# A small load, read by nothing, issued on SP just ahead of the last store

## The chip, the cores and the metric

The kernel runs on one core of one Trainium2 chip. The metric is device time in microseconds (us) per execution. Most figures below are medians of several executions; single traces are named as such. Every execution quoted here is of the fast state. The ratio of two kernels is the mean time of one kernel's fast runs over that of the other's of the same rounds, so it is not quite the ratio of the medians quoted beside it. SP, DVE and ACT are the engines SyncE, VectorE and ScalarE. In the traces a transfer shows as packets and as sixteen completions on its semaphore (the store of the kernel before: 144 packets, completions from 82.429 to 82.597 us); it is counted as landed at the last of the sixteen.

## The reference

```python
batch, dim = 1024, 4096          # x and y: float32
def reference(x, y, axis):       # axis = -1
    return np.sum((x - y) ** 2, axis=axis).astype(np.float32)
```

33.5 MB are read, 4 KB are written: 1024 sums, which stand as 8 sums on each of 128 partitions.

## The kernel before

SP issues all transfers. The two inputs are loaded in slices that get smaller towards the end; DVE subtracts, ACT squares and sums, and the very last 128 columns are squared and summed on DVE. When DVE has reduced the last partial sums (semaphore `sums`), SP stores all 1024 results in one transfer, clears the semaphores while it is under way (81.577 to 81.645 us in the trace, with the store landing at 82.597), and waits for it (semaphore `stored`). Shortened, with comments added:

```python
class Program:
    ...
    def close(self, engine, stored, value):
        engine.sem_clear(range(self.sems[0].num, self.sems[-1].num + 1))
        engine.wait_ge(stored, value).then_inc(stored, -value)
...
    for j, (c0, c1) in enumerate(ys):
        final = j == len(ys) - 1
        wait_loaded(c1, landed_y[j][1])
        for piece in pieces_of(j, c0, c1):
            sub(*piece)                                   # DVE, then_inc(diffs, 1)
            if final:
                nc.vector.wait_ge(diffs, n["diffs"])
                nc.vector.tensor_tensor_reduce(...).then_inc(sums, 1)
                ...
            square(*piece, where[piece])                  # ACT
    ...
    complete(7)                                           # DVE reduce, then_inc(sums, 1)

    nc.sync.wait_ge(sums, n["sums"])
    nc.sync.dma_start(out=ov, in_=results).then_inc(stored, 16)
    prog.close(nc.sync, stored, 16)
```

## Time and profile before

| What | us | From |
|---|---|---|
| median of the first three executions | 83.98 (83.97 to 84.12) | times |
| span of the profiled execution | 82.63 | trace |
| last load landed | 80.251 | semaphore records |
| last sum ready | 81.161 | semaphore records |
| store issued | 81.177 to 81.525 | trace |
| store's first and last packet | 82.019, 82.213 | DMA packet records |
| store's last completion | 82.597 | semaphore records |

The table is read downwards: the last sum is ready, and the store takes 1.42 us from its issue to its last completion. The lines of the profile that show this stand in the prediction.

### The profile page before, as it was taken

How to read it: one execution, taken by the hardware profiler on the slowest of the kernel's cores; microseconds unless marked ns; L12 is line 12 of the kernel's file. 1: busy time of each engine (PE TensorE's matmuls, PEld its weight loads, DVE VectorE, ACT ScalarE, POOL GpSimd, SP SyncE). 2: the span in 40 equal slices, each digit the busy share in tenths (PEclk: the TensorE clock that was granted, in tenths of full speed). 3: DMA queues.
4: the chain of work that ended last, by engine and by line, in shares of the span. 5: the costliest groups of instructions: out<-in, count | busy, mean ns of one | idle time of the engine just before them, and what ended most of it. 6: DMA issues, size and time to landing. Idle time of an engine off the chain costs nothing.

```text
span 82.6 us, 136 instructions
## 1 busy us (share of the span) xinstructions
DVE 36.8 (45%) x27; ACT 33.4 (40%) x41; POOL 0.2 (0%) x4
## 2 busy tenths in 40 slices
DVE  0000000000000000000299999999189996989992
ACT  3300000000000000000000979889896999899991
POOL 0000000000000000000000000000000000000000
DMA  5998998888999991999599699969979799999960
GB/s 127 389 500 381 595 547 381 381 381 381 504 504 504 504 504 63 441 504 504 254 508 508 286 476 508 476 286 508 423 339 509 339 437 440 426 402 416 395 220 2
DMA packets 2736, 33.56 MB, mean 406 GB/s; under 512 B 432, under 2 KB 1328, under 8 KB 1712
## 3 DMA queue, kind: packets, MB, share of 16 engines
q1 hardware_dynamic: 2736, 33.56, 95.9%
HBM read 33.55 MB, written 0.00 MB: 406 GB/s over the span
## 4 chain that ended last, share of the span: by engine, by line
DMA 63%; SPq 16%; DVE 12%; ACT 4%; issue 1%
DMA Y<-in_y_dram 63%; SPq L108 16%; DVE X L175 11%; ACT X L181 4%; DVE Y L204 0%; DVE results L188 0%; SPq L220 0%; DVE results L204 0%
## 5 line engine op out<-in xcount | busy, mean ns | idle before, releaser
L175 DVE TENSOR_TENSOR X<-X,Y 128x2048 f32<-128x2048 f32 (+10 forms) x21 | 36.2, 1780 | 44.3 <-DMA Y<-in_y_dram 44.3
L181 ACT ACTIVATE X<-X 128x2048 f32<-128x2048 f32 (+9 forms) x20 | 31.2, 1559 | 46.1 <-DVE X L175 46.0
L181 ACT ACTIVATION_READ_ACCUMULATOR X<-X 128x1 f32 x20 | 3.7, 186 | 0.0
L181 ACT ACT_TABLE_LOAD x1 | 1.3, 1283 | 1.4 <-PEq L19 1.4
L188 DVE TENSOR_REDUCE results<-parts 128x1 f32<-128x2 f32 (+2 forms) x4 | 0.4, 152 | 0.0
L204 DVE CUSTOM_DVE_ANT_0 Y<-X,parts 128x128 f32<-128x128 f32 x1 | 0.4, 352 | 0.0
L250 POOL MEMSET const-bfloat16-1.0<- 128x1 bf16 x1 | 0.1, 101 | 0.0
L250 POOL MEMSET const-uint8-127<- 128x1 uint8 x1 | 0.1, 101 | 0.0
L250 POOL MEMSET const-float32-0.0<- 128x1 f32 x1 | 0.1, 98 | 0.2 <-issue 0.2
L250 POOL MEMSET const-float32-1.0<- 128x1 f32 x1 | 0.1, 98 | 0.0
L204 DVE DVE_READ_ACCUMULATOR2_ANT results<- 128x1 f32 x1 | 0.1, 83 | 0.0
## 6 DMA issues: line engine op xcount, KB each, us to landing
Y<-in_y_dram SPq DMA_DIRECT2D x1, 8128.0 KB, 39.0
X<-in_x_dram SPq DMA_DIRECT2D x1, 6144.0 KB, 20.2
X<-in_x_dram SPq DMA_DIRECT2D x1, 4096.0 KB, 48.3
Y<-in_y_dram SPq DMA_DIRECT2D x1, 4096.0 KB, 57.5
X<-in_x_dram SPq DMA_DIRECT2D x1, 2736.0 KB, 13.3
X<-in_x_dram SPq DMA_DIRECT2D x1, 2048.0 KB, 7.1
Y<-in_y_dram SPq DMA_DIRECT2D x1, 1392.0 KB, 19.0
Y<-in_y_dram SPq DMA_DIRECT2D x1, 1312.0 KB, 16.1
```

The costliest lines, as they stand in the source:

```text
L108: nc.sync.dma_start(out=dst[:, home(c0, c1)], in_=src[:, c0:c1]).then_inc(sem, 16)
L175: nc.vector.tensor_sub(out=a, in0=a, in1=Y[:, home(c0, c1)]).then_inc(diffs, 1)
L181: nc.scalar.activation(out=a, in_=a, func=Square, accum_out=acc).then_inc(acts, 1)
L188: nc.vector.tensor_reduce(out=results[:, r : r + 1], in_=parts_of(r, len(row_parts[r])), axis=mybir.AxisListType.X, op=add,).then_inc(sums, 1)
L204: nc.vector.tensor_tensor_reduce(out=Y[:, home(*piece)], in0=X[:, home(*piece)], in1=X[:, home(*piece)], scale=1.0, scalar=parts_of(r, 1), ...
L250: nc = _bacc.Bacc("TRN2", target_bir_lowering=False, num_devices=1)
```

## The change

The intent is to have the DMA queue at work just before the store that the kernel ends with, so that the store doesn't begin on a queue that has fallen idle (for 2.15 us in the trace of before, 79.872 to 82.019). SP waits for the last subtraction, issues a load of 32 bytes per partition into a buffer that nothing reads, and then waits for the sums as before. The load has a semaphore of its own, which is waited for and reset at the end.

```diff
+        self.own = []
...
         engine.sem_clear(range(self.sems[0].num, self.sems[-1].num + 1))
+        for sem in self.own:
+            engine.wait_ge(sem, value).then_inc(sem, -value)
         engine.wait_ge(stored, value).then_inc(stored, -value)
...
     stored = nc.alloc_semaphore("stored")
+    prog.own.append(nc.alloc_semaphore("ahead"))
...
+    ahead = nc.alloc_sbuf_tensor("ahead_home", [P, R], F32).ap()
+    nc.sync.wait_ge(diffs, n["diffs"])
+    nc.sync.dma_start(out=ahead, in_=xv[:, 0:R]).then_inc(prog.own[0], 16)
     nc.sync.wait_ge(sums, n["sums"])
     nc.sync.dma_start(out=ov, in_=results).then_inc(stored, 16)
```

## The prediction

> **What bounds the kernel now.** I read the page first (busy shares, the 40 slices), then the chain that ended last, then the timeline of the last three microseconds, the stretches of that tail, SP's own waits, and finally the single records of DMA packets and semaphore updates in the trace, because the chain stops before the store.
>
> From the page:
>
> ```profile
> DVE 36.8 (45%) x27; ACT 33.4 (40%) x41; POOL 0.2 (0%) x4
> ...
> DMA  5998998888999991999599699969979799999960
> ...
> q1 hardware_dynamic: 2736, 33.56, 95.9%
> ```
>
> The DMA row is full almost to the end, DVE and ACT are below half. The kernel is a stream of 33.55 MB at a mean of 406 GB/s; nothing that SP adds after the last load can touch that stream. Only the last two slices (2.07 us each) are not DMA-bound, and there the change sits.
>
> The end of the chain that ended last (start us, us, what):
>
> ```profile
> 66.94 13.12 DMA Y<-in_y_dram
> 80.05 0.02 issue
> 80.08 0.57 DVE X L175 x2
> 80.65 0.03 issue
> 80.67 0.35 DVE Y L204
> 81.03 0.01 DVE results L204
> 81.03 0.12 DVE results L188
> ```
>
> The last load lands at 80.05, two subtractions end at 80.65, a multiply-and-sum and a reduction follow. The chain leaves out the store; the timeline and the list of DMA issues have it:
>
> ```profile
> 81.18 0.35 SPq L232 DMA_DIRECT2D out_dram<-results  x1
> ```
> ```profile
> out_dram<-results SPq DMA_DIRECT2D x1, 4.0 KB, 1.4
> ```
>
> So the span of 82.63 us ends with 1.4 us of one 4 KB store. The stretches of the tail show that almost none of it is data (columns: stretch, its length, busy DVE, ACT, POOL, clock, DMA share, GB/s):
>
> ```profile
> 79.90:81.20 1.30, 1.18 (x6) 1.06 (x6) 0.00 (x0) 1.00 0.00 0
> 81.20:82.00 0.80, 0.00 (x0) 0.00 (x0) 0.00 (x0) 1.00 0.00 0
> 82.00:82.25 0.25, 0.00 (x0) 0.00 (x0) 0.00 (x0) 1.00 0.31 17
> 82.25:82.63 0.38, 0.00 (x0) 0.00 (x0) 0.00 (x0) 1.00 0.00 0
> ```
>
> The trace's records refine this. Last reduction's update 81.161; store issued 81.177 to 81.525; first of its 144 packets (128 of 32 B, 16 of 4 B) at 82.019, sixteen of them begun within 25 ns; last at 82.213; sixteen completions from 82.429 to 82.597; SP's closing wait passes at 82.613 and ends at 82.630. The store is therefore 0.842 us from issue to first packet, 0.20 us of packets, 0.38 us to the last completion. The DMA engines stood empty from 79.872 to 82.019, that is 2.15 us. The load can only help by shortening the 0.842 us: that is where a queue that has gone idle would pay.
>
> [...]
>
> **The change part by part.** It removes nothing. It adds on SP a wait for the last subtraction, one load issue of 4 KB (128 rows of 8 f32), and after the clearing of semaphores one more wait-and-subtract. It moves nothing.
>
> 1. The load's issue. The last subtraction's update comes at 80.648. SP took 16 ns from the sums' update (81.161) to the store's issue (81.177), so the load starts at about 80.664. What does an issue take? From the timeline:
>
> ```profile
> 53.45 0.33 SPq L108 DMA_DIRECT2D X<-in_x_dram  x1
> 53.82 0.91 SPq L108 DMA_DIRECT2D Y<-in_y_dram  x2
> 54.77 0.44 SPq L108 DMA_DIRECT2D X<-in_x_dram  x1
> ```
>
> One issue after a pause takes 0.33 us, the following ones 0.43 to 0.44, and they end about 0.48 us apart. [...] The load ends on SP at 80.664 + 0.33 = 80.99; with the 0.05 us that lie between two issues SP is at the store by 81.04, before the sums at 81.161. Slack 0.12 us; with 0.44 us instead, SP is ready at 81.15 and the slack is 10 ns.
>
> [...]
>
> 3. The load's packets. Issue to first packet as for the store, 0.84 us: 81.51. Packets 0.20 us if like the store's: 81.71. Completions up to 0.58 us after the first packet: about 82.09. The store's packets, due at 82.02, find an engine that finished the load's data 0.3 us before. So they do not collide[...].
>
> 4. The extra closing wait. SP clears semaphores at 81.577 to 81.645, then waits for the load (about 82.09) and then for the store (82.597). The first wait ends 0.5 us before the second could; its 17 ns and the gap are beside the store. Cost 0.
>
> 5. DVE and ACT: no instruction changed. The load writes a buffer of its own from 81.5 on, when both are done.
>
> Sum of the costs: 0 on the path. The gain is whatever part of 0.842 us belongs to an idle queue. What can it be? [...] 0.842 - 0.48 = 0.36 us remain, an upper bound. A second view: the very first load, at 0.00 us, with the queue unused before, has its first packet at 0.998, which is 0.156 us more than the store had after 2.15 us of pause. So a colder queue seems slower, but this shows only the step from unused to 2 us idle, not from 2 us to 0.3 us. I choose about a quarter of the 0.36 us, 0.08 us, as an estimate: no trace here shows that a gain of this kind exists, yet one piece of evidence leans that way.
>
> Predicted: 83.98 - 0.08 = 83.90 us.
>
> **The rivals.**
>
> - Nothing is cold. 0.842 us is the fixed length of an issue, and the store lands 1.4 us after 81.18 as before. For it: sixteen packets of the store begin within 25 ns[...]. Against it: the 0.998 us of the first load, whose packets also begin up to 0.5 us apart. Time 83.98, within the scatter of 83.97 to 84.12. This is the single most likely outcome.
> - The queue[...] is cold and the load wakes it. The store then starts 0.2 to 0.36 us earlier: 83.6 to 83.8. For it: 2.15 us of emptiness[...]. Against it: nothing in this trace shows a small DMA on a warm queue.
> - The load gets in the way. [...] the first packets of the first load took 0.92 to 1.43 us where the later ones of the same 16 KB took 0.611, so a first read can cost 0.3 to 0.8 us more. Added to the load's start at 81.51 this reaches 81.8 to 82.5, and the store would begin up to 0.3 us late after 82.02; the extra wait for the load would then also be close to the end. Time 84.1 to 84.3. Against it: those first packets met sixteen engines starting on 16 KB each at once, this load has 32 B each.
> - The load lands after the store and its wait becomes the end. It would need more than 1.93 us from 80.664 to 82.597, where the store needed 1.42. [...] time at most some 0.2 us more.
>
> **Range and chances.** The gain is bounded by 0.36 us and the plausible losses by about 0.3 us. I give the first rival some 45 in 100, a gain of over 0.1 us some 35, a loss of over 0.1 us some 20. The scatter between runs is up to 0.14 us. This gives 83.60 to 84.22 us. Two per cent are 1.68 us, more than the store's whole 1.4 us: faster by so much is practically excluded, 0.01; slower by so much would need an effect that nothing in the profile hints at, 0.015; within 2% 0.975.
>
> **What would show each step right or wrong.** In the profile of the changed kernel: a load issue on SP at 80.66 of about 0.33 us (step 1); the store's issue still 16 ns after the sums and 0.33 to 0.36 us long (steps 1 and 2), not 0.43 or later; a group of 144 packets between 81.5 and 81.75 that is separate from the store's (step 3); the load's wait closing before 82.2 (step 4). The verdict between the rivals is one number: the store's first packet relative to its issue. 0.84 us means that nothing was cold, 0.5 to 0.75 that the load woke the queue, more than 0.84 that it stands in the way. The prediction is wrong if the time leaves 83.60 to 84.22, and its reasoning is wrong, even inside the range, if the time moves while the store's issue-to-landing stays 1.4 us.

The forecast's sum came to 83.98 - 0.08 = 83.90 us: costs of 0 on the path, and a gain of 0.08 us as about a quarter of 0.842 - 0.48 = 0.36 us. Terms of this sum rested on mechanisms and figures that no trace shows: step 2 of the costs (expected delay 0, at worst some 0.1 us), the same delay among the losses of the third rival, and the reason for taking 0.48 us off the 0.842 us. What the trace shows of the 0.48 us is that the ends of successive issues lie so far apart; that every store has to wait so long before its first packet was my assumption.

## The result and the profile after

In the first comparison the changed kernel took 84.21 us (median of 6, 84.11 to 84.68) and the kernel before 84.06 us (median of 6, 83.97 to 84.12): ratio 1.0028, 95% interval 1.0005 to 1.0052. Predicted were 83.90 us and a small gain. There was no gain. The median lies just inside the upper end of the range, 84.22; the mean of the six, 84.29, lies outside. Of the 0.31 us between 83.90 and 84.21, 0.08 us are the gain that isn't there, 0.08 us the starting point (83.98 was a median of three executions, six gave 84.06), and 0.15 us the difference of this comparison.

The page of the changed kernel, its DMA row in 40 slices and its DMA queue:

```profile
DMA  5999999888999997599799979979999999999950
...
q1 hardware_dynamic: 2880, 33.56, 95.7%
```

The stream is as full as before (95.7% and 95.9% of the span); the 144 packets more are the small load. Next its timeline at the end, and the list of its DMA issues (KB each, us from issue to landing):

```profile
80.91 0.33 SPq L238 DMA_DIRECT2D ahead_home<-in_x_dram  x1
81.42 0.35 SPq L240 DMA_DIRECT2D out_dram<-results  x1
```
```profile
ahead_home<-in_x_dram SPq DMA_DIRECT2D x1, 4.0 KB, 1.7
out_dram<-results SPq DMA_DIRECT2D x1, 4.0 KB, 1.4
```

The load is where it was meant to be, and its issue takes 0.33 us. The store still needs 1.4 us; by the semaphore records it is 81.417 to 82.829, that is 1.412 us, against 1.420 before. The number that the prediction had named, issue to first packet, is 0.842 us as before. (The records don't name the transfer of a packet, and a few of the load's come late in this trace; n1_again below, where the two groups are apart, has 0.840 us.) The stretches of this tail (stretch, length, busy DVE, ACT, POOL, clock, DMA share, GB/s) have the same form as before, except that most of the small load's packets now lie in the first of them:

```profile
81.42:82.25 0.83, 0.00 (x0) 0.00 (x0) 0.00 (x0) 1.00 0.08 5
82.25:82.46 0.21, 0.00 (x0) 0.00 (x0) 0.00 (x0) 1.00 0.39 21
82.46:82.87 0.41, 0.00 (x0) 0.00 (x0) 0.00 (x0) 1.00 0.00 0
```

So where do the 0.23 us come from by which this span (82.863 us) is longer than that of before (82.630 us)? The chain that ended last answers, in its last pieces (start us, us, what):

```profile
67.24 13.06 DMA Y<-in_y_dram
...
80.32 0.57 DVE X L179 x2
...
81.28 0.11 DVE results L192
```

The last load lands at 80.30 here by this view and at 80.05 there, on the transfer that the chain follows (the last but one; the very last landed at 80.476 and 80.251). All that follows is shifted by that quarter of a microsecond. The small load is issued at 80.912, when the stream is done (last landing at 80.476); it can't have delayed it. One more sight of the profile matters, SP's own waits (line, what for, us, times, longest):

```profile
SPq L47 <- SPq L47: 0.8, 1, 0.8
...
SPq L48 <- SPq L48: 0.2, 1, 0.2
```

L47 is the new closing wait for the load, L48 the one for the store. SP waits 0.8 us for the load and then only 0.2 us for the store. The load is thus much closer to setting the end than the prediction had it: its last completion came at 82.644, the store's at 82.829.

### The profile page after: what moved, and what is told of

Read it like the earlier page. It is cut to its first block, busy times and chain, and to the rows that moved or that the text cites. A ratio compares the mean times of both kernels' runs of the same rounds, so it can differ in the third digit from the quotient of the medians.

```text
span 82.9 us, 138 instructions
## 1 busy us (share of the span) xinstructions
DVE 36.8 (44%) x27; ACT 33.4 (40%) x41; POOL 0.2 (0%) x4
## 3 DMA queue, kind: packets, MB, share of 16 engines
q1 hardware_dynamic: 2880, 33.56, 95.7%
## 4 chain that ended last, share of the span: by engine, by line
DMA 63%; SPq 16%; DVE 12%; ACT 4%; issue 1%
DMA Y<-in_y_dram 63%; SPq L112 16%; DVE X L179 11%; ACT X L185 4%; DVE Y L208 0%; DVE results L192 0%; SPq L224 0%; DVE results L208 0%
```

## The experiments

Three theories were put against each other. A: nothing was cold, the load is off the path, and the difference of the first comparison is scatter of the load stream. B: the shifted semaphore numbers or the layout of the program slow the stream. C: in some executions the small load lands after the store and sets the end.

### n0_numbers: the numbering alone

```diff
     stored = nc.alloc_semaphore("stored")
+    nc.alloc_semaphore("ahead")
...
+    nc.alloc_sbuf_tensor("ahead_home", [P, R], F32).ap()
     nc.sync.wait_ge(sums, n["sums"])
```

> The kernel before with the change's extra semaphore and extra buffer allocated, but no load and no wait. Theory A (the load is off the path; the 0.15 us between the medians is skew between the DMA engines that stands before any changed instruction and differs from execution to execution or chip to chip): ratio to before 1.000, within 0.001. Theory B (the shifted semaphore numbers or layout slow the load stream): ratio about 1.002 to 1.003, with the sixteen completions of the first load spread over some 0.55 us as in the profile of the changed kernel, not 0.23 us as in that of before. Theory C (the small load lands after the store in some executions): 1.000.

Measured: 84.09 us (84.05 to 84.24), before 84.06 us; ratio 1.0002, interval 0.9988 to 1.0015. Its trace has a wide spread in the first load's completions (0.521 us from the first to the last of the sixteen; 0.226 us in the trace of before, 0.577 us in that of the changed kernel) and a last load at 80.441 us, although the time equals that of before. So the late stream that I saw in the changed kernel's trace also comes in a kernel without the load, and the wide spread in it does not mark a slower kernel. No slowing by the numbers shows; an effect below about 0.15% would not be seen. The added instructions are not in this kernel; for them the repeats of the changed kernel stand.

### n1_again: the changed kernel on the same chip

No edit.

> The changed kernel again, on the same chip as the other runs of this call. Theory A: ratio 1.000 to 1.001, no skewed tail of slow executions, and the spread of the first load's completions as in the other runs of this chip. Theory B: 1.002 to 1.003 and a wide spread of 0.55 us, like n0_numbers. Theory C: 1.001 to 1.003 with single executions 0.3 to 0.6 us slow, while the quickest executions equal those of before; the small load's last completion within 0.2 us of the store's.

Measured: 84.15 us (83.95 to 84.38); ratio 1.0004, interval 0.9987 to 1.0021. The quickest execution, 83.95, is as quick as the kernel before on that chip (83.96), and the 0.28% did not come back. In this trace the packets of load and store are cleanly apart: the store's first is 0.840 us after its issue. The load's last completion lies 0.363 us ahead of the store's. One execution at 84.38 left theory C open.

### e1_early: the load two subtractions earlier

```diff
-    nc.sync.wait_ge(diffs, n["diffs"])
+    nc.sync.wait_ge(diffs, n["diffs"] - 2)
```

> The same load, issued two subtractions earlier, some 0.6 us sooner, so that its landing can't set the end. Issue to landing of the store stays 1.41 to 1.42 us in all theories but a warm queue. Theory A: 1.000. Theory B: 1.002 to 1.003, as n1_again. Theory C: 1.000, and without the slow executions that n1_again has.

Measured: 84.12 us (84.05 to 84.32); ratio 1.0006, interval 0.9991 to 1.0021. Store: 0.843 us to the first packet, 1.420 us to landing. The load itself was issued at 80.210, only 0.24 us after the last packet of the stream (79.971), and its first packet came 0.934 us after its issue; in the changed kernel, where the pause ahead of the load's issue was 0.75 us, it took 0.929 us. A shorter pause did not help the load.

### e2_two: two loads ahead of the store

```diff
     nc.sync.dma_start(out=ahead, in_=xv[:, 0:R]).then_inc(prog.own[0], 16)
+    nc.sync.dma_start(out=ahead2, in_=xv[:, R:2 * R]).then_inc(prog.own[1], 16)
```

(The second load has its own buffer and semaphore.)

> Two such loads one after the other before the store[...]. If[...] nothing is cold, the store's issue ends 0.44 us later than it would, its first packet stays 0.49 us after the end of the issue, and the time is 0.40 to 0.48 us more than before (ratio 1.005). If a queue with work standing on it starts the store sooner, the first packet comes less than 0.40 us after the end of the issue and the ratio is under 1.003. In theory C the second load, landing 1.73 us after an issue at 81.04, ends at 82.8 and still lies before the store.

(The 0.44 us expected here rest on the 0.48 us between the ends of successive issues in the trace of before.)

Measured: 84.59 us; ratio 1.0062, interval 1.0047 to 1.0077. The timeline of its end, and the store in its list of issues:

```profile
80.77 0.33 SPq L239 DMA_DIRECT2D ahead_home<-in_x_dram  x1
81.14 0.43 SPq L241 DMA_DIRECT2D ahead_home<-in_x_dram  x1
81.62 0.43 SPq L243 DMA_DIRECT2D out_dram<-results  x1
```
```profile
out_dram<-results SPq DMA_DIRECT2D x1, 4.0 KB, 1.6
```

Here is what was measured with work standing on the queue: the store's issue took 0.43 us, and the three issues ended 0.475 us apart (81.098, 81.573, 82.047 us). With the 0.926 us that lie between the last load's landing and the store's issue in the trace of before, this store would have been issued at 81.258 and done at 81.606; it is late by 0.441 us. The remainder is behind the issue: 1.168 us from its end to landing and not 1.072 us, so 0.10 us more. The sum, 0.54 us, is what the trace shows (2.917 us from the last load's landing to the end of the span, against 2.379 us) and a little more than I had expected, 0.40 to 0.48 us. The records don't name the transfer of a packet; those of the second load and of the store touch here, and the second load's last completion (83.046) comes only 0.17 us before the store's (83.215). What the 0.10 us are was not shown.

### e3_behind: the load behind the store

```diff
+    nc.sync.wait_ge(sums, n["sums"])
+    nc.sync.dma_start(out=ov, in_=results).then_inc(stored, 16)
     nc.sync.dma_start(out=ahead, in_=xv[:, 0:R]).then_inc(prog.own[0], 16)
-    nc.sync.wait_ge(sums, n["sums"])
-    nc.sync.dma_start(out=ov, in_=results).then_inc(stored, 16)
```

(The wait for `diffs` goes too.)

> The small load issued right behind the store instead of ahead of it, so that its landing is certain to set the end: what the load costs where it isn't hidden. Its issue starts about 0.40 us after the store's and lands 1.54 to 1.73 us after that, as the two profiles of the changed kernel had it, so the end moves from 1.42 us after the store's issue to about 1.95 to 2.15 us: 0.53 to 0.73 us more, ratio 1.006 to 1.009. The store itself still lands 1.41 to 1.42 us after its issue. If a small load behind a store lands as quickly as a store, the ratio is 1.005.

Measured: 85.02 us (84.91 to 85.6); ratio 1.0122, interval 1.0091 to 1.0152. From its list of issues:

```profile
out_dram<-results SPq DMA_DIRECT2D x1, 4.0 KB, 1.4
ahead_home<-in_x_dram SPq DMA_DIRECT2D x1, 4.0 KB, 1.8
```

The store still lands 1.412 us after its issue; the load, issued 0.391 us after it, took 1.810 us, and the second closing wait passed 0.08 us after the first. From the store's issue to the end of the span it is 2.313 us, against 1.453 us before: 0.86 us more. I expected at most 0.73 us, because I took the load's landing to be 1.54 to 1.73 us and forgot that the second wait comes after the first. So when the load isn't hidden it costs most of a microsecond. In the changed kernel it is hidden, by a margin of 0.2 to 0.4 us.

This trace and that of e2_two also show a load issued while another transfer stands on the queue. Counted from the end of its issue, its first packet came after 0.602 us here (82.098 to 82.700) and after 0.599 us for the second load of e2_two (81.573 to 82.172); behind the pause of the changed kernel it was 0.601 us (81.240 to 81.841). A busy queue did not start the load sooner; only its issue was longer, 0.43 us and not 0.33 us.

### e4_idle: a long pause before the store

```diff
     complete(7)
+    for i in range(7):
+        a0 = X[:, 2048 * i : 2048 * (i + 1)]
+        nc.vector.wait_ge(acts, n["acts"])
+        last_sub = nc.vector.tensor_sub(out=Y[:, 2048 * i : 2048 * (i + 1)], in0=a0, in1=a0)
+    last_sub.then_inc(sums, 1)
+    n["sums"] += 1
```

> No small load; seven subtractions of 128x2048 on buffers that are no longer needed delay the store by some 16 us, so that the queue is empty for 18 us and not 2.15 us before it. If an idle queue is never slower at these lengths, issue to first packet stays 0.84 us and issue to landing 1.41 to 1.42 us. If idleness costs and 2.15 us is simply too short to show it, issue to first packet is 0.95 us or more. The time is some 16 us more in both; only the interval is of interest.

Measured: 99.41 us, as the added DVE work would have it. The stretches from the end of the stream on, and the store's issue in the timeline:

```profile
81.00:96.60 15.60, 15.57 (x9) 0.00 (x0) 0.00 (x0) 1.00 0.00 0
96.60:97.43 0.83, 0.00 (x0) 0.00 (x0) 0.00 (x0) 1.00 0.00 0
97.43:97.64 0.21, 0.00 (x0) 0.00 (x0) 0.00 (x0) 1.00 0.37 20
```
```profile
96.59 0.35 SPq L238 DMA_DIRECT2D out_dram<-results  x1
```

The DMA engines had been empty for 17.6 us (79.860 to 97.438). The store took 0.843 us to its first packet and 1.410 us to landing, as after 2.15 us of emptiness. So a pause of 17.6 us cost nothing over one of 2.15 us (0.843 and 0.842 us). Whether the store is quicker on a queue in use, this run can't show; the changed kernel does, and it is not: in n1_again the load's packets end 0.11 us before the store's begin, and the store took 0.840 us to its first packet.

### e5_split and e6_half: half the rows

If nothing is cold, what are the 0.84 us made of? I had assumed that 0.48 us of them, the distance between the ends of successive issues, grow with the 128 rows; no trace shows that. Then fewer rows should start sooner, and two halves on two queues would beat both kernels. (The first two outcomes below are for this assumption, with the time for the rows passing on each queue by itself in the first and on the two queues one after the other in the second.)

```diff
-    nc.sync.dma_start(out=ov, in_=results).then_inc(stored, 16)
-    prog.close(nc.sync, stored, 16)
+    nc.scalar.wait_ge(sums, n["sums"])
+    nc.sync.dma_start(out=ov[0:64], in_=results[0:64]).then_inc(stored, 16)
+    nc.scalar.dma_start(out=ov[64:128], in_=results[64:128]).then_inc(stored, 16)
+    nc.scalar.wait_ge(sums, n["sums"]).then_inc(acted, 1)
+    nc.sync.wait_ge(acted, 1).then_inc(acted, -1)
+    prog.close(nc.sync, stored, 32)
```

(The line that allocates `acted` is left out. This semaphore only sees to it that SP doesn't clear `sums` while ACT may still be waiting for it.)

> No small load; the store is cut in two halves of 64 rows, one issued by SP and one at the same time by ACT. [...] both halves have their first packet about 0.60 us after the issue and the time is 0.2 us less (ratio 0.997 to 0.998). [...] the second half comes at 0.84 us and the ratio is 1.000. If the 0.84 us doesn't depend on the rows, or if ACT's queue, unused until then, starts later, the ratio is 1.000 to 1.003.

Measured for e5_split: 84.70 us (84.66 to 84.88); ratio 1.0076, interval 1.0062 to 1.0090. It is slower, which none of the outcomes that I had written down allows.

```diff
-    nc.sync.dma_start(out=ov, in_=results).then_inc(stored, 16)
+    nc.sync.dma_start(out=ov[0:64], in_=results[0:64]).then_inc(stored, 16)
```

> Only the first 64 rows are stored, by SP; the result is wrong on purpose (the other 512 sums are not written). [...] issue to first packet falls from 0.84 to about 0.60 us and the time by 0.24 us (ratio 0.997); if the interval is fixed per DMA, 0.84 us and ratio 1.000.

Measured for e6_half (result wrong): 84.39 us; ratio 1.0045, interval 1.0023 to 1.0067. Both expectations fail again: the one of 0.60 us, which rested on the same assumption, and the one of 0.84 us. Its store in the timeline and in the list of issues, and then the two stores of e5_split in its list:

```profile
81.30 0.52 SPq L232 DMA_DIRECT2D out_dram<-results  x1
```
```profile
out_dram<-results SPq DMA_DIRECT2D x1, 2.0 KB, 1.7
```
```profile
out_dram<-results SPq DMA_DIRECT2D x1, 2.0 KB, 1.7
out_dram<-results ACTq DMA_DIRECT2D x1, 2.0 KB, 2.0
```

A store of 64 rows took longer to issue (0.523 us) than one of 128 rows (0.348 us) and had its first packet 1.168 us after its issue and not 0.842 us. In e5_split the two halves were issued within 5 ns of each other, and the second group of 80 packets began 0.27 us after the first (82.531 and 82.800). The two queues did not start side by side; the last completion was 1.961 us after the issue. Why 64 rows were slower than 128 stays open. What follows is only that my division of the 0.84 us into 0.48 us for 128 rows and 0.36 us for waking was not a measurement of anything; what the 0.84 us are made of stays open too.

### e7_big: a larger load ahead of the store

```diff
-    ahead = nc.alloc_sbuf_tensor("ahead_home", [P, R], F32).ap()
+    ahead = nc.alloc_sbuf_tensor("ahead_home", [P, 512], F32).ap()
...
-    nc.sync.dma_start(out=ahead, in_=xv[:, 0:R]).then_inc(prog.own[0], 16)
+    nc.sync.dma_start(out=ahead, in_=xv[:, 0:512]).then_inc(prog.own[0], 16)
```

> The load ahead of the store with 2 KB in each row (256 KB) and not 32 B, all else equal: from when on does it stand in the store's way? An estimate: the stream moved 16 engines' 33.55 MB at 406 GB/s, so 256 KB take 0.65 us; its packets run from 0.93 us after its issue (81.75) to about 82.4, where the store's would begin at 82.15 to 82.26. If the store has to wait its turn behind them, the store lands 0.15 to 0.4 us later than 1.42 us after its issue and the ratio is 1.002 to 1.005; if store and load share the engines freely, issue to landing of the store stays below 1.5 us, and the load's own landing at about 82.9 to 83.0 sets the end (ratio 1.002 to 1.004).

Measured: 84.98 us (84.86 to 85.06); ratio 1.0108, interval 1.0094 to 1.0123. From its list of issues:

```profile
ahead_home<-in_x_dram SPq DMA_DIRECT2D x1, 256.0 KB, 2.6
...
out_dram<-results SPq DMA_DIRECT2D x1, 4.0 KB, 2.3
```

The store, issued at its normal point, landed after 2.263 us, 0.84 us later than usual, and after the load (83.484 and 83.330). I expected at most 0.4 us. At 2 KB per row the load ahead did stand in the store's way; load and store together ran from 81.655 to 83.057. My estimate of 0.65 us for 256 KB took the stream's rate; the packets of this short transfer took 1.35 us (81.655 to 83.008), so it was about half as fast, 194 GB/s against 406. The 32 bytes per row of the change did no such harm.

### n2_before, n3_after, n4_after: controls

No edit in any of them: the first is the kernel before, the others are the changed kernel.

> The kernel before, unchanged, as a control: how far two runs of one kernel differ on one chip, and a second trace of it. Theory A (the tail is as long with the load as without; what differs is when the load stream ends, already decided in its first load): ratio 1.000 within 0.002; last load's landing 80.25 to 80.50 and the rest of the span after it 2.34 to 2.39 us, as in all traces so far. If the last load again lands at 80.25 here while n3_after and n4_after have 80.40 or more, the change has a hand in the stream after all.

> The changed kernel a third time. Theory A: ratio 1.000 to 1.001; span after the last load's landing 2.34 to 2.39 us; the 1.0028 of the first comparison does not come back. If the change has a small cost of its own outside the path that the traces show: 1.002 to 1.003 again.

> The changed kernel a fourth time, for the same question: ratio 1.000 to 1.001 in theory A, 1.002 to 1.003 if it has a cost of its own; together with n3_after it shows how far two runs of one kernel lie apart.

Measured: n2_before 84.11 us, ratio 1.0004 (0.9989 to 1.0019); n3_after 84.17 us, ratio 1.0010 (0.9997 to 1.0023); n4_after 84.06 us, ratio 1.0004 (0.9987 to 1.0021). The chain of n2_before is the best single picture, because it lies beside that of the changed kernel shown above:

```profile
67.20 13.10 DMA Y<-in_y_dram
...
81.28 0.14 DVE results L188
```

The kernel before reaches its last reduction at 81.28 us here, the time of the changed kernel's first trace, and not at 81.03 as in its own first trace. Two executions of one kernel thus lie further apart than the two first traces did, and the quarter of a microsecond needs no effect of the change. What makes a stream end late was not found. One half of theory A as I had written it falls, though: whether the stream ends late isn't always decided in the first load. n3_after had its first load done by 7.120 us, as early as before (7.117), and its last at 80.451.

### n5_after, n6_after, e8_early, e9_early: the slow single executions

No new edit: the changed kernel twice and e1_early twice. Theory C was still possible: by then 4 of 23 executions of the changed kernel had taken over 84.30 us (84.36, 84.36, 84.38, 84.68), and no execution of the kernel before had.

> The changed kernel again, for its slow single executions: so far 4 of 23 took over 84.30 us (84.36, 84.36, 84.38, 84.68), none of 42 of the kernel before. If they are the small load landing after the store (theory C), about one in six does so here too, and the trace shows the load's last completion somewhere within 0.4 us of the store's. If they are chance, none or one in five or six executions, and the ratio is 1.000 to 1.001.

> The load two subtractions earlier, as in e1_early: it lands some 0.8 us before the store and can hardly set the end. Theory C: no execution over 84.30 us. If the slow ones come from having the load at all, or by chance, they appear here as often as in the changed kernel (e1_early had 1 of 6).

> As n5_after, to raise the count: theory C about one in six over 84.30 us; chance, none or one. Ratio 1.000 to 1.001 unless slow executions are among them.

> As e8_early, to raise the count: theory C none over 84.30 us; otherwise as often as n5_after and n6_after.

Measured: n5_after 84.06 us, ratio 0.9995 (0.9979 to 1.0012), slowest 84.17; n6_after 84.13 us, ratio 1.0002 (0.9986 to 1.0017), slowest 84.19; e8_early 84.15 us, ratio 1.0006 (0.9988 to 1.0023), slowest 84.28; e9_early 84.12 us, ratio 1.0003 (0.9990 to 1.0017), slowest 84.19. No execution of the late load was over 84.30 us here, where theory C asked for about two of twelve. One of 18 executions of the early load was (84.32), where theory C asked for none. Both speak against C, but weakly: with so few executions neither excludes it. In all six traces of the changed kernel the small load's last completion lies before the store's, by 0.19 to 0.39 us. What made single executions slow, 84.68 us among them, was not caught in a trace and stays open. In all runs together 4 of 35 executions of the changed kernel and none of 43 of the kernel before took over 84.30 us, so a rare cost of the change is not excluded.

## Why the prediction was wrong

The predicted gain of 0.08 us is not there: five repeats of the changed kernel gave 1.0004, 1.0010, 1.0004, 0.9995 and 1.0002 of the kernel before. No single repeat excludes a gain of 0.1% by its interval. What excludes it is the store itself: in all nine traces of the changed kernel and of e1_early it takes 1.407 to 1.420 us from issue to landing, and without a load ahead 1.409 to 1.420 us. The first comparison's 1.0028 was the largest of six draws; two of its six executions were over 84.30 us. The prediction's own sign of wrong reasoning, a time that moves while the store keeps its 1.4 us, was there in that comparison; in the repeats the time does not move.

Here are five traces with the change or a neighbour of it beside three without (us):

| Trace | last load lands | store: issue to first packet | store: issue to landing | last load's landing to end of span |
|---|---|---|---|---|
| before | 80.251 | 0.842 | 1.420 | 2.379 |
| n2_before | 80.500 | 0.846 | 1.418 | 2.406 |
| n0_numbers | 80.441 | 0.845 | 1.409 | 2.359 |
| the change, first trace | 80.476 | 0.842 | 1.412 | 2.387 |
| n1_again | 80.419 | 0.840 | 1.415 | 2.340 |
| n6_after | 80.468 | 0.841 | 1.410 | 2.350 |
| e1_early | 80.383 | 0.843 | 1.420 | 2.391 |
| e8_early | 80.432 | 0.844 | 1.407 | 2.357 |

The third and fourth columns don't show whether a load went ahead. The second varies by 0.25 us, in one and the same kernel too, and with it the span.

**The step that failed** is the sum of the gain: "about a quarter of the 0.36 us, 0.08 us". Both of its supports fall.

- "the very first load [...] has its first packet at 0.998, which is 0.156 us more than the store had after 2.15 us of pause. So a colder queue seems slower." This compared a load with a store. The small load on a queue in use has its first packet 0.93 us after its issue (0.929 in the changed kernel, 0.934 in e1_early, with pauses of 0.75 and 0.24 us), so 0.09 of the 0.156 us stand between a load and a store of like size in traces in which the queue has been in use. The other 0.07 us may belong to a queue never used before or to rows of 16 KB; no run separates these. The like-for-like comparison is e4_idle: 0.843 us after 17.6 us of emptiness, 0.842 us after 2.15 us.
- "0.842 - 0.48 = 0.36 us remain, an upper bound." The 0.48 us were a distance between successive issues, and e2_two confirms that distance (0.475 us). But that this time is inside the 0.842 us, in proportion to the rows, was my assumption; half the rows took 1.168 us. The remainder had no meaning as a share of waking.

**The first rival, "nothing is cold", was right**, and the prediction called it the single most likely outcome. I set the point estimate below it all the same, because I held a gain of over 0.1 us to be likelier than such a loss.

**The steps of the costs.** Step 1 held: issue of the load of 0.328 us, SP free in time, the store's issue 16 ns after the sums (81.401 and 81.417) and 0.348 us long, so that the delay of step 2 was 0 as well. In e7_big the store landed 0.15 us after the load that was issued first, 2.263 us after its issue, while nothing but the load had changed. Step 3 was too favourable: the packets took longer than the store's 0.20 us (0.28 us in n1_again, 81.746 to 82.030), and they run up to the store's; in three of the six traces of the changed kernel (n3_after, n4_after, n5_after) no gap of even 0.09 us is left between the two groups, and in the first one 137 packets came before the gap and 151 after it, so seven of the load's were late. The store's landing was not moved by this. Step 4 had the right verdict, cost 0, from a wrong size: 1.43 us to the load's landing was expected, 1.53 to 1.73 us were measured in the six traces (1.732 in the first), and the margin was 0.19 to 0.39 us and not 0.5 us. e3_behind shows what is lost when this margin is used up. Two readings were off without bearing on the result: 80.05 is the landing of the last load but one, and the first sixteen packets of the first load took 0.96 to 1.43 us, not from 0.92 us on.

**The other rivals.** "The load gets in the way" didn't happen at 32 bytes per row (the store took 1.410 to 1.415 us in three traces of the changed kernel), and did with a second load (0.54 us) or with 2 KB per row (0.84 us). "The load lands after the store" was not seen in any of six traces.

What remains is a change without a benefit and with a thin margin. If it costs anything in the mean, that is at the limit of what these runs can show: the repeats lie between 0.9995 and 1.0010, the unchanged kernel against itself at 1.0004. None of the runs beats either kernel.

## What to carry to other kernels

Before something is warmed, measure the same transfer after a long pause, after a short one and right behind another transfer; a first load was no stand-in for the last store here (0.998 us to the first packet against 0.842). Compare the interval that a change aims at, here the store's issue to landing, and not the spans of two single traces, which differ by a quarter of a microsecond by themselves. A transfer ahead of the last store was harmless here only as long as its issue, nearly all of its packets and its landing fitted in front of the store's, and each of the three has its own size: 0.33 us, 0.28 us (n1_again) and 1.53 to 1.73 us from the issue.
